# The gate stage of a fused two-model kernel: paced by VectorE's work, shorter look-ups, one-hots shared with ScalarE, and masks added on VectorE

## The chip, the cores and the metric

The kernel runs on one core of one Trainium2 chip. The metric is the device time of one execution in microseconds (us). The kernel before took 3335.89 us as the median of three runs (3335.77 to 3343.4). Every line number "L..." is a line of the kernel before, if nothing else is said.

## The reference

512 tokens of width 1024 pass through five blocks: a mixer of a state-space branch and a forgetting attention, a PEER feed-forward, an even mixer (sparse and differential attention), an odd mixer (compressed, selected and sliding-window attention) and two SwiGLU feed-forwards behind the last two mixers. Two places matter here.

The PEER block scores 8 heads of 2 x 128 keys, takes the best 16 of each half, then the best 16 of the 256 sums, and mixes 128 of 16384 experts per token:

```python
s_top, i_top = lax.top_k(scores, PEER_TOPK)
cand_s = (s_top[..., 0, :, None] + s_top[..., 1, None, :]).reshape(...)
cand_i = (i_top[..., 0, :, None] * PEER_KEYS + i_top[..., 1, None, :]).reshape(...)
best_s, pos = lax.top_k(cand_s, PEER_TOPK)
expert_idx = jnp.take_along_axis(cand_i, pos, axis=-1)
gates = jax.nn.softmax(best_s, axis=-1)
...
act = jax.nn.gelu(jnp.einsum('td,thkd->thk', h_blk, u_sel))
w = (g_blk * act)
return jnp.einsum('thk,thkd->td', w, v_tab[i_blk])
```

The two attentions with plain causal masks are the differential one of the even mixer and the two key branches of the odd one: `s = jnp.where(causal, s, -inf)`, a softmax over the row, and a product with the values.

## The kernel before, in words

Each stream of weights comes in tiles of 128x1024 (512 KB) through one class, `Stream` (from L55 on): a load on SP's queue (L67), a high part of reduced precision made by ScalarE (L75) and the rest made by VectorE (L76). A product is three matmuls, high x high, low x high and high x low (`mm3`, L327 to L330). The program is handed to a scheduler that orders each engine's instructions; every engine then works off its own order.

**PEER** (`peer`, from L932 on). Token block 0 (128 tokens) takes its 128 experts' rows by indirect DMA, one row per token at a time (`gathered`, L967 to L993: POOL issues, VectorE multiplies and sums). The other three blocks (384 tokens) go through all 16384 experts densely, 128 experts at a time: a u pass (`u_pass`, L961) is 24 matmuls over 384 columns that give the activations of 128 experts, and a v pass (`v_pass`, L1182) is 18 matmuls over 512 columns that add their share to the output. Between them the activation is multiplied by the gates, which are zero for all but the chosen experts.

Stage by stage:

- *Query stage.* 16 products, the scores, and `top16` on VectorE.
- *Gate stage.* The first N_SPILL = 80 u passes run ahead of any gate; their activations are parked in DRAM (`spill`, L1132; Gelu on ScalarE at L1138, store at L1140). Beside the first 72 of them the gates are made, in steps of a generator (`all_gates`, L1110): `prep` (L1022) makes for a block of tokens the 50 candidates that can be among the best 16 (their sums `cs` and numbers `ci`), takes the best 16 per head, and looks the numbers up. For the look-up VectorE compares 50 candidates x 16 places (`eq`, L1064), multiplies by the numbers (`pk`, L1066) and sums over the candidates (`ei`, L1067). `build` (L1091) then makes the dense gates, four tokens in a step: one-hots of the second half-key `o2` (L1099) and of the first one times the gate `og` (L1101), both on VectorE, four multiplications of 128x128 on TensorE (L1105), a copy on ScalarE (L1106); a store of 2 MB after each eight steps (L1108). After each parked pass three steps of the generator are taken (`tick`, GATE_RATE = 3), and a step of `all_gates` takes one of `build` and one of `prep` together. Gathers come by `tick(1, ...)`: up to DOTS_C = 20 of 260 in the gate stage.
- *The last eight parked passes* run in the next pools; then come the v passes, 0 to 127. Parked activations and gates are loaded again (L1156), multiplied on POOL (L1163), split (L1166, L1167). Passes 0 to 76 are v passes alone; from there on a u pass stands before each v pass (`peer_order`, L45). The gathers go on beside them at a rate of R_SPILL = 0.7 in the first 80 entries of the order and 1.0 after that.

**Masks.** In `diff_first` (even mixer, L1462; 32 row blocks) and `first` (odd mixer, L1809; 128 row blocks) a row block of scores is two products into one PSUM bank, and between them a third matmul adds the causal mask: identity x mask, in bf16 (L1472, L1819). VectorE takes the negative maximum of the row (L1475, L1821), ScalarE the exponential straight from PSUM (L1477, L1823), and the bank is free after that. The forgetting attention of the first mixer uses another form: one fused operation of VectorE that negates the scores' sum with a second operand and takes the extreme of the row at once, with the sum written to SBUF (L851).

## Time and profile before

| | |
|---|---|
| runs | 3335.77, 3335.89, 3343.4 us |
| the profiled execution | 3341.76 us, its span 3339.6 us |
| TensorE (PE) busy | 3171.5 us, 95% |
| VectorE (DVE) busy | 2242.3 us, 67% |
| ScalarE (ACT) busy | 1345.7 us, 40% |
| GpSimd (POOL) busy | 680.9 us, 20% |
| mean granted clock of TensorE | 0.977 |
| read from HBM, written to it | 474.17 MB, 51.40 MB |

A busy TensorE is not one at its peak: its matmuls are pipelined and their ends are modelled, so rates are read from the starts of rows. Busy shares over the whole span hide the stages; the gate stage lies at about 592 to 1008 us of the span, the v passes from 1050 to about 1800, the even mixer's first attention at about 1920 to 2060 and the odd mixer's at about 2670 to 2940.

### The profile page before, as it was taken

To read this page: it belongs to the slowest core of one execution; us is meant where nothing else is said; L and a number is where in the kernel's file an instruction comes from. 1 tells how busy PE (TensorE), PEld (TensorE's weight loads), DVE (VectorE), ACT (ScalarE), POOL (GpSimd) and SP (SyncE) were. 2 spreads that over 40 slices of the span, in tenths; PEclk is the share of its full clock that TensorE was granted. 3 is DMA by queue.
4 is the path that set the end of the run, shared out by engine and by line. 5 is a ranking of instruction groups with operands and counts; after the bars stand their busy time and mean duration, and the time that the engine had idled before them with its cause. 6 is when DMAs were issued, how large, how long until landed. Compare 5 with 4: busy or idle time off the path is not lost.

```text
span 3339.6 us, 46326 instructions
## 1 busy us (share of the span) xinstructions
PE 3171.5 (95%) x17267; PEld 2759.1 (83%) x17267; DVE 2242.3 (67%) x4704; ACT 1345.7 (40%) x2494; POOL 680.9 (20%) x815
## 2 busy tenths in 40 slices
PE   7989999988999999999999997999999999999999
PEld 6988878988998777899998985878888986778887
DVE  6886349999985787888887787643324377753322
ACT  4445333423443333333334455632322377742322
POOL 1451000010004555566673100000000110000000
PEclk9999999999999999999999997999999998999999
DMA  4223232455669999999997230123233210123232
GB/s 140 79 78 113 95 120 81 154 189 199 237 249 345 321 354 319 319 345 335 340 332 249 70 101 16 42 82 101 95 95 121 83 45 4 55 65 100 95 95 82
DMA packets 226418, 529.25 MB, mean 158 GB/s; under 512 B 19081, under 2 KB 113161, under 8 KB 224273
## 3 DMA queue, kind: packets, MB, share of 16 engines
q1 hardware_dynamic: 186448, 376.32, 33.4%
q0 software_dynamic: 36864, 134.23, 11.2%
q10 hardware_dynamic: 2880, 15.73, 1.2%
q8 instruction: 136, 2.23, 0.3%
q14 instruction: 90, 0.73, 0.1%
HBM read 474.17 MB, written 51.40 MB: 157 GB/s over the span
## 4 chain that ended last, share of the span: by engine, by line
PE 75%; DVE 15%; ACT 3%; DMA 3%; issue 2%; POOL 1%; SPq 0%; ACTq 0%; DVEq 0%; POOLq 0%
PE mm L329 20%; PE mm L328 20%; PE mm L330 19%; DVE wlo L76 3%; PE ax L1105 2%; PE ax L328 2%; PE ax L330 2%; PE ax L329 2%; DMA wraw<-in_peer_v_dram 1%; PE tx L1280 1%; ACT whi L75 1%; DVE ei L1067 1%; PE tx L1840 1%; DVE xn L319 1%; DMA rw<-in_peer_rows_dram,idx 1%
## 5 line engine op out<-in xcount | busy, mean ns | idle before, releaser
L76 DVE TENSOR_TENSOR wlo<-wraw,whi 128x1024 fp32r<-128x1024 f32 x525 | 670.3, 1277 | 573.2 <-ACT whi L75 565.9
L75 ACT CAST whi<-wraw 128x1024 fp32r<-128x1024 f32 x525 | 549.5, 1049 | 1042.3 <-PE mm L329 402.6
L330 PE MATMUL mm<-hhi,wlo 128*128 128x512 f32 (+2 forms) x1608 | 600.0, 374 | 10.2 <-DVE wlo L76 10.1
L328 PE MATMUL mm<-hhi,whi 128*128 128x512 f32 (+2 forms) x1608 | 602.1, 375 | 0.3 <-ACT whi L75 0.3
L329 PE MATMUL mm<-hlo,whi 128*128 128x512 f32 (+2 forms) x1608 | 600.9, 374 | 0.0
L328 PE MATMUL mm<-whi,hhi 128*128 128x256 f32 (+1 forms) x1280 | 382.7, 300 | 9.4 <-DVE vl L272 4.5
L330 PE MATMUL mm<-whi,hlo 128*128 128x256 f32 (+1 forms) x1280 | 380.3, 299 | 3.0 <-DVE hlo L272 2.7
L329 PE MATMUL mm<-wlo,hhi 128*128 128x256 f32 (+1 forms) x1280 | 381.6, 299 | 0.0
L330 PEld LDWEIGHTS mm<-hhi,wlo 128*128 128x128 f32 (+1 forms) x1608 | 303.6, 189 | 52.7 <-DVE wlo L76 12.0
L328 PEld LDWEIGHTS mm<-hhi,whi 128*128 128x128 f32 (+1 forms) x1608 | 304.1, 189 | 41.7 <-ACT hhi L271 0.7
L329 PEld LDWEIGHTS mm<-hlo,whi 128*128 128x128 f32 (+1 forms) x1608 | 303.6, 189 | 40.7 <-DVE hlo L272 0.4
L329 PE MATMUL mm<-wlo,wth 128*128 128x512 f32 x768 | 304.7, 397 | 1.2 <-DVE wlo L76 0.8
L330 PE MATMUL mm<-whi,wtl 128*128 128x512 f32 x768 | 303.6, 395 | 0.0
L975 POOL DMA_INDIRECT rw<-in_peer_rows_dram,idx x128 | 169.9, 1328 | 634.5 <-DVE act L984 377.3
L328 PE MATMUL mm<-whi,wth 128*128 128x512 f32 x768 | 250.8, 400 | 24.0 <-ACT whi L75 24.0
L328 PEld LDWEIGHTS mm<-whi,hhi 128*128 128x128 f32 x1280 | 248.3, 194 | 17.9 <-DVE vl L272 4.7
L330 PEld LDWEIGHTS mm<-whi,hlo 128*128 128x128 f32 x1280 | 246.8, 193 | 9.8 <-DVE hlo L272 3.0
L329 PEld LDWEIGHTS mm<-wlo,hhi 128*128 128x128 f32 x1280 | 248.2, 194 | 6.2 <-issue 0.2
L975 POOL DMA_INDIRECT rw<-in_peer_v_dram,idx x128 | 179.8, 1405 | 96.2 <-DVE acc L992 72.2
L328 PEld LDWEIGHTS mm<-whi,wth 128*128 128x128 f32 x768 | 145.1, 190 | 60.5 <-ACT whi L75 29.8
L1166 ACT CAST wth<-w 128x384 fp32r<-128x384 f32 x128 | 65.8, 514 | 285.4 <-PE mm L329 198.2
L992 DVE SCALAR_TENSOR_TENSOR acc<-rw,act,acc 128x1024 f32<-128x1024 f32 x127 | 176.4, 1389 | 5.7 <-DMA rw<-in_peer_v_dram,idx 4.5
(558 smaller groups left out, 5903.4 us busy)
## 6 DMA issues: line engine op xcount, KB each, us to landing
wraw<-in_peer_u_dram SPq DMA_DIRECT2D x128, 512.0 KB, 4.5
wraw<-in_peer_v_dram SPq DMA_DIRECT2D x128, 512.0 KB, 6.9
gt<-gst SPq DMA_DIRECT2D x12, 2048.0 KB, 7.2
g<-gt SPq DMA_DIRECT2D x32, 768.0 KB, 10.0
wraw<-in_w_gate_dram SPq DMA_DIRECT2D x44, 512.0 KB, 3.4
wraw<-in_w_up_dram SPq DMA_DIRECT2D x44, 512.0 KB, 3.5
wraw<-in_w_down_dram SPq DMA_DIRECT2D x44, 512.0 KB, 3.7
at<-as ACTq DMA_DIRECT2D x20, 768.0 KB, 5.0
```

What stands on the lines that cost most here:

```text
L75: self.nc.scalar.copy(hi[:, :w], r[:, :w])
L76: self.last = self.nc.vector.tensor_sub(lo[:, :w], r[:, :w], hi[:, :w])
L319: V.scalar_tensor_tensor(xn, x[:, o], rs, grow[:, o], op0=ALU.mult, op1=ALU.mult)
L328: PE.matmul(ps, ah, bh, start=start, stop=False)
L329: PE.matmul(ps, ah, bl, start=False, stop=False)
L330: PE.matmul(ps, al, bh, start=False, stop=stop)
L975: G.indirect_dma_start(out=rw, out_offset=None, in_=A[("peer_rows", "peer_v")[m]], in_offset=bass.IndirectOffsetOnAxis(ap=idx[:, k:k + 1], ...
L992: V.scalar_tensor_tensor(acc0, rw, act[:, k:k + 1], acc0, op0=ALU.mult, op1=ALU.add)
L1067: V.tensor_reduce(ei[:, hd], pk.rearrange("p c k -> p k c"), axis=AX.X, op=ALU.add)
L1105: PE.matmul(ps[:, i * P:(i + 1) * P], o2[:, i], og[:, i], start=True, stop=True)
L1166: S.copy(wh, w)
L1280: K["nc"].tensor.transpose(ps[:, t * P:(t + 1) * P], src(t), K["ident"])
```

## The change

1. N_SPILL goes from 80 to 72, so that 64 passes stand in the gate stage and eight more u passes beside v passes. DOTS_C goes from 20 to 28 and R_SPILL from 0.7 to 0.62.
2. A step of the generator now says how much it weighs (1 to 4), `build` and `prep` steps count one by one, and after each parked pass as much weight is taken as spreads all of it over the 64 passes.
3. The look-up of the first eight of 16 places compares only 20 candidates, the second eight all 50: 560 elements instead of 800. The numbers are copied to that list by ScalarE (`cl`, seven copies per block of tokens), and the product is written with the candidates in order, so that the sum reads them in order.
4. Two of four `og` per step are made by ScalarE: an Abs of the difference and a Relu of gate minus gate x difference. The slots are copied by ScalarE, and the negated gate is made by VectorE.
5. The mask matmuls go; VectorE adds the mask in the fused operation and writes the sum to SBUF, and the exponential works there in place. The mask is made once per mixer by POOL and VectorE.

```diff
-N_SPILL = 80
-GATE_RATE = 3
-DOTS_C = 20
+N_SPILL = 72
+DOTS_C = 28
-R_SPILL = 0.7
+R_SPILL = 0.62
...
+            FEW = [(sum(PAIRS[:a]), 8 // (a + 1), 1) for a in range(4)]
+            FEW += [(sum(PAIRS[:4]), 1, 1), (sum(PAIRS[:5]), 3, PAIRS[5])]
+            NF8 = sum(n for _, n, _ in FEW)
+            NL = NF8 + NC
...
-                yield
+                cl = tp.tile([P, 8, NL], F32, tag="cl", bufs=1, name=nm("cl"))
+                lists(S.copy, cl, ci)
+                yield 4
...
-                    eq = tp.tile([P, NC, TOPK], BF16, tag="eq", bufs=1, name=nm("eq"))
-                    V.tensor_tensor(eq, iox, bcast(bp[:, hd], 1, NC), op=ALU.is_equal)
-                    pk = tp.tile([P, NC, TOPK], F32, tag="pk", bufs=1, name=nm("pk"))
-                    V.tensor_mul(pk, eq, bcast(ci[:, hd], 2, TOPK))
-                    V.tensor_reduce(ei[:, hd], pk.rearrange("p c k -> p k c"), axis=AX.X, op=ALU.add)
-                    yield
+                    eq = tp.tile([P, NL, 8], BF16, tag="eq", bufs=1, name=nm("eq"))
+                    pk = tp.tile([P, 8, NL], F32, tag="pk", bufs=1, name=nm("pk"))
+                    halves = [(slice(0, NF8), slice(0, 8)), (slice(NF8, NL), slice(8, 16))]
+                    for c, k in halves:
+                        V.tensor_tensor(eq[:, c], iox[:, c], bcast(bp[:, hd, k], 1, c.stop - c.start), op=ALU.is_equal)
+                    V.tensor_mul(pk.rearrange("p k c -> p c k"), eq, bcast(cl[:, hd], 2, 8))
+                    for c, k in halves:
+                        V.tensor_reduce(ei[:, hd, k], pk[:, :, c], axis=AX.X, op=ALU.add)
+                    yield 2
...
-                sl = tp.tile([P, 3, P], F32, tag="sl", bufs=2, name=nm("sl"))
-                V.tensor_copy(sl.rearrange("p a b -> p (a b)"), ps[:, :3 * P])
-                yield
+                sl = tp.tile([P, 4, P], F32, tag="sl", bufs=2, name=nm("sl"))
+                S.copy(sl[:, :3].rearrange("p a b -> p (a b)"), ps[:, :3 * P])
+                V.tensor_scalar(sl[:, 3], ps[:, 2 * P:3 * P], -1.0, None, op0=ALU.mult)
+                yield 2
...
                         for i in range(4):
-                            V.tensor_scalar(og[:, i], iot, sl[:, 0, t0 + i:t0 + i + 1], sl[:, 2, t0 + i:t0 + i + 1],
-                                            op0=ALU.is_equal, op1=ALU.mult)
+                            e, g, ng = (sl[:, q, t0 + i:t0 + i + 1] for q in (0, 2, 3))
+                            if i % 2:
+                                ds = tp.tile([P, P], F32, tag="ds", bufs=2, name=nm("ds"))
+                                S.activation(ds, iot, AF.Abs, bias=e, scale=-1.0)
+                                S.activation(og[:, i], ds, AF.Relu, bias=g, scale=ng)
+                            else:
+                                V.tensor_scalar(og[:, i], iot, e, g, op0=ALU.is_equal, op1=ALU.mult)
...
-                        yield
+                        yield 1.25
...
                         for g in list(both):
-                            if next(g, 0) == 0:
+                            n = next(g, 0)
+                            if n == 0:
                                 both.remove(g)
-                        yield
+                            else:
+                                yield n
...
+            work = NT * (4 + 8 + 2 + 16) + ND * (2 + 32 * 1.25)
             for e in range(N_SPILL - N_LATE):
                 spill(e, tp)
-                tick(0, GATE_RATE * (e + 1))
+                tick(0, work * (e + 1) / (N_SPILL - N_LATE))
                 tick(1, (e + 1) * DOTS_C // N_SPILL)
...
+def causal_mask(K, pool):
+
+    mk = pool.tile([P, T], F32, name=K["nm"]("mk"))
+    K["nc"].gpsimd.memset(mk[:, :T - P], 0.0)
+    K["nc"].vector.tensor_copy(mk[:, T - P:], K["tri"])
+    return mk
...
                 PE.matmul(ps[:, :N], qr, kh[:, :N], start=True, stop=False)
-                PE.matmul(ps[:, W - P:W], identb, trib, start=False, stop=False)
                 PE.matmul(ps[:, :N], qr, kl[:, :N], start=False, stop=True)
-                V.tensor_reduce(mx[:, r:r + 1], ps[:, :W], axis=AX.X, op=ALU.max, negate=True)
                 p = op.tile([P, W], F32, tag=f"pd{r}", bufs=3 if r > 1 else 2, name=nm("pd"))
-                S.activation(p, ps[:, :W], AF.Exp, bias=mx[:, r:r + 1], accum_out=den[:, r:r + 1])
+                V.tensor_tensor_reduce(p, ps[:, :W], mk[:, T - W:], -1.0, 3.0e38, op0=ALU.add, op1=ALU.min,
+                                       accum_out=mx[:, r:r + 1])
+                S.activation(p, p, AF.Exp, bias=mx[:, r:r + 1], scale=-1.0, accum_out=den[:, r:r + 1])
```

The same edit of the masks is made in `diff_first`.

Three places of the order show how the instructions stand. Lines of the changed kernel are its own: L74 is the split of L75, L1126 the Abs, L1127 the Relu, L1132 the one-hot multiplication of L1105, L1133 the copy of L1106, L1169 the Gelu of L1138.

ScalarE among the one-hot steps, before:

```order
L1106 COPY gst_8048<-ax_8251 128x128x4
L1106 COPY gst_8048<-ax_8269 128x128x4
L75 CAST whi_9924<-wraw_9831 128x1024
L1138 ACTIVATE as_9857<-mm_9891 128x384
L1106 COPY gst_8313<-ax_8321 128x128x4
L1106 COPY gst_8313<-ax_8339 128x128x4
L75 CAST whi_9960<-wraw_9864 128x1024
L1138 ACTIVATE as_9857<-mm_9923 128x384
```

ScalarE at the like place now:

```order
L1126 ACTIVATE ds_9131<-iot,sl_8276 128x128
L1126 ACTIVATE ds_9135<-iot,sl_8276 128x128
L1127 ACTIVATE og_9128<-ds_9131,sl_8276 128x128
L1127 ACTIVATE og_9128<-ds_9135,sl_8276 128x128
L1133 COPY gst_9046<-ax_9058 128x128x4
L1126 ACTIVATE ds_9191<-iot,sl_8276 128x128
L1126 ACTIVATE ds_9195<-iot,sl_8276 128x128
L74 CAST whi_9463<-wraw_9276 128x1024
L1169 ACTIVATE as_9302<-mm_9401 128x384
L1127 ACTIVATE og_9188<-ds_9191,sl_8276 128x128
L1127 ACTIVATE og_9188<-ds_9195,sl_8276 128x128
```

Between two splits of a weight tile ScalarE had a Gelu and two or three copies; now each step brings two Abs and two Relu as well, and some Relu stand behind the next split and the next Gelu.

TensorE at the last one-hot steps, before: they end inside the third last pass of the loop, and two whole passes and the eight late ones follow.

```order
L328 MATMUL mm_10524<-hhi_5370,whi_10456 128x384
L329 MATMUL mm_10524<-hlo_5371,whi_10456 128x384
L1105 MATMUL ax_9706<-og_9700,o_1168_9699 128x128 x4
L330 MATMUL mm_10524<-hhi_5370,wlo_10457 128x384
L328 MATMUL mm_10524<-hhi_5370,whi_10456 128x384
L329 MATMUL mm_10524<-hlo_5371,whi_10456 128x384
L330 MATMUL mm_10524<-hhi_5370,wlo_10457 128x384
L1105 MATMUL ax_9719<-og_9713,o_1171_9712 128x128 x4
L328 MATMUL mm_10524<-hhi_5370,whi_10456 128x384
```

TensorE at the end of the loop now (39 one-hot multiplications stand behind the last pass mm_10788; the first twelve rows from its last matmul on):

```order
L329 MATMUL mm_10788<-hhi_5370,wlo_10619 128x384
L1132 MATMUL ax_10611<-og_10601,o_1351_10600 128x128 x3
L1132 MATMUL ax_10660<-og_10650,o_1357_10649 128x128
L1132 MATMUL ax_10679<-og_10669,o_1363_10668 128x128
L1132 MATMUL ax_10660<-og_10650,o_1357_10649 128x128 x3
L1132 MATMUL ax_10679<-og_10669,o_1363_10668 128x128 x2
L1132 MATMUL ax_10696<-og_10686,o_1368_10685 128x128
L1132 MATMUL ax_10679<-og_10669,o_1363_10668 128x128
L1132 MATMUL ax_10748<-og_10738,o_1375_10737 128x128
L1132 MATMUL ax_10696<-og_10686,o_1368_10685 128x128 x2
L1132 MATMUL ax_10765<-og_10755,o_1380_10754 128x128
L1132 MATMUL ax_10696<-og_10686,o_1368_10685 128x128
```

Before, every one-hot step had matmuls of a pass behind it; now the last ten stand by themselves. From the first of the 384 one-hot multiplications to the last there are 910 matmuls of passes before (37.9 passes) and 835 now (34.8), and 29 whole passes stand ahead of the first one now.

TensorE at a row block of scores in the odd mixer, before:

```order
L1818 MATMUL sx_25321<-kdh_24446,qs_24601 128x256
L1819 LDWEIGHTS identb
L1819 MATMUL sx_25321<-trib,identb 128x128
L1820 MATMUL sx_25321<-kdl_24447,qs_24601 128x256
L1818 MATMUL sx_25328<-kdh_24446,qs_24601 128x384
```

and now:

```order
L1860 MATMUL sx_26585<-kdh_25104,qs_25322 128x512
L1861 MATMUL sx_26585<-kdl_25105,qs_25322 128x512
L1860 MATMUL sx_26636<-kdh_25141,qs_25322 128x256
L1861 MATMUL sx_26636<-kdl_25142,qs_25322 128x256
L1882 MATMUL tx_26556<-ident,pd_26443 128x128
```

Two instructions of TensorE's queue are gone per row block.

## Rows read from the trace of the kernel before

**Rows 1.** The page, part 4: the chain of work that ended last, by engine.

```profile
PE 75%; DVE 15%; ACT 3%; DMA 3%; issue 2%; POOL 1%; SPq 0%; ACTq 0%; DVEq 0%; POOLq 0%
```

**Rows 2.** Busy time by stretch: length, busy us (instructions) per engine, clock, DMA share, GB/s.

```profile
core 0: us, PE busy (x) PEld busy (x) DVE busy (x) ACT busy (x) POOL busy (x), PEclk, DMA share, GB/s
592.00:1008.00 416.00, 397.61 (x2505) 393.72 (x2504) 392.70 (x1081) 171.37 (x254) 26.27 (x19) 0.98 0.59 209
...
725.00:1008.00 283.00, 272.24 (x1800) 269.05 (x1799) 266.67 (x667) 119.15 (x185) 16.18 (x11) 0.98 0.61 220
1050.00:1394.00 344.00, 325.66 (x1374) 257.84 (x1373) 268.09 (x326) 112.22 (x151) 198.24 (x162) 1.00 0.94 335
1394.00:1792.00 398.00, 398.00 (x2002) 360.88 (x2001) 333.82 (x309) 142.70 (x192) 265.40 (x193) 1.00 0.94 335
1920.00:2060.00 140.00, 110.52 (x653) 93.79 (x652) 119.15 (x313) 68.15 (x178) 9.27 (x12) 0.82 0.19 64
2670.00:2940.00 270.00, 254.57 (x1607) 200.01 (x1607) 205.12 (x470) 197.38 (x523) 15.29 (x20) 0.96 0.10 34
```

**Rows 3.** Line 1138, the Gelu: ns min/median/max, first and last start.

```profile
L1138 ACT ACTIVATE as<-mm x72: 476/483/496, 597.1 to 1003.8; 128x384 f32<-128x384 f32 x72
```

**Rows 4.** Timeline of TensorE in a pass: start us, us, engine, line, operation.

```profile
871.50 1.05 PE L1105 MATMUL ax<-og,o 128*128 128x128 f32 x8
...
872.31 0.42 PE L330 MATMUL mm<-hhi,wlo 128*128 128x384 f32 x1
...
873.09 0.34 PE L328 MATMUL mm<-hhi,whi 128*128 128x384 f32 x1
...
875.69 0.33 PE L328 MATMUL mm<-hhi,whi 128*128 128x384 f32 x1
```

**Rows 5.** Groups by line, 592 to 1008 us: count | busy us, mean ns | idle before.

```profile
L1101 DVE TENSOR_SCALAR og<-iot,sl 128x128 f32<-128x128 f32 x384 | 106.4, 339 | 0.0
L76 DVE TENSOR_TENSOR wlo<-wraw,whi 128x1024 fp32r<-128x1024 f32 x72 | 87.8, 1221 | 11.6 <-ACT whi L75 11.6
...
L1067 DVE TENSOR_REDUCE ei<-pk 128x16 f32<-128x800 f32 x32 | 49.5, 1547 | 0.1
L1066 DVE TENSOR_TENSOR pk<-eq,ci 128x800 f32<-128x800 bf16 x32 | 31.7, 992 | 0.1
L1064 DVE TENSOR_TENSOR eq<-iox,bp 128x800 bf16<-128x800 bf16 x32 | 18.3, 571 | 0.0
...
L75 ACT CAST whi<-wraw 128x1024 fp32r<-128x1024 f32 x72 | 75.7, 1052 | 129.5 <-PE mm L329 107.6 <-DMA wraw<-in_peer_u_dram 9.2 <-PE ax L1105 6.8
L1106 ACT COPY gst<-ax 128x512 f32<-128x512 f32 x96 | 56.2, 586 | 104.2 <-PE ax L1105 104.0
```

**Rows 6.** ScalarE: group of line 853; timeline of two neighbours in the late passes.

```profile
L853 ACT ACTIVATE prow<-prow,mx 128x128 f32<-128x128 f32 x8 | 3.2, 403 | 5.0 <-DVE mx L851 5.0
...
1006.96 1.05 ACT L75 CAST whi<-wraw 128x1024 fp32r<-128x1024 f32 x1 [2.72 <-PE ax L329]
1007.92 0.49 ACT L1138 ACTIVATE as<-ax 128x384 f32<-128x384 f32 x1
```

**Rows 7.** DMA from 1050 to 1394 us, all queues.

```profile
DMA packets 54356, 115.24 MB, mean 335 GB/s; under 512 B 3228, under 2 KB 30876, under 8 KB 54335
```

**Rows 8.** Groups by line, 2670 to 2940 us: a maximum over 512 elements in order.

```profile
L1821 DVE TENSOR_REDUCE mx<-sx 128x1 f32<-128x512 f32 x32 | 22.0, 687 | 11.2 <-PE sx L1820 11.0
```

**Rows 9.** Odd mixer: timeline of TensorE; its wait for the score bank (us, times, longest).

```profile
2829.26 0.28 PE L1818 MATMUL sx<-kdh,qs 128*128 128x256 f32 x1
...
2829.62 0.28 PE L1818 MATMUL sx<-kdh,qs 128*128 128x256 f32 x1
...
2830.22 0.28 PE L328 MATMUL mm<-whi,hhi 128*128 128x256 f32 x1
...
2830.34 0.28 PE L329 MATMUL mm<-wlo,hhi 128*128 128x256 f32 x1
...
PE sx L1818 <- ACT pd L1823: 5.7, 11, 1.1
```

**Rows 10.** Line 851, the fused operation of the first mixer: its accumulator read.

```profile
L851 DVE DVE_READ_ACCUMULATOR2_ANT mx<- x32: 71/82/85, 91.6 to 327.1; 128x1 f32 x32
```

More of the change, by code (lines that the diff above doesn't have):

```diff
@@ L1127, in tick @@
                     with tc.issue_after(ws.last.ins) if lane else nullcontext():
-                        if next(lanes[lane], 0) == 0:
-                            lanes[lane] = None
-                    done[lane] += 1
+                        n = next(lanes[lane], 0)
+                    if n == 0:
+                        lanes[lane] = None
+                    done[lane] += n
             def spill(e, pool, bank=bank_m):
```

34 lines of the change are left out of this document (22 added, 12 removed).

## Prediction

> **What bounds the kernel now.** Start with the chain of work that ended last: three quarters of the span is TensorE [rows 1]. So a microsecond counts only if it is taken from TensorE's instructions or from a gap between them, and the busy time by stage tells where gaps are [rows 2]. Four stages matter.
>
> Gate stage (parked passes, 592 to 1008 us): TensorE is busy for 397.6 us and VectorE for 392.7 of 416, while ScalarE has 171.4 [rows 2]. The Gelu that ends a parked pass starts first at 597.1 and for the 72nd time at 1003.8 [rows 3]: 71 intervals of 5.73, about 412 us for 72. What must TensorE do in them? The starts from 873.09 to 875.69 are 15 steps of 0.173, and a pass has 24 matmuls: 4.16 us. One one-hot step (four multiplications, shown as eight) holds the queue from 871.50 to 872.31, 0.81 us [rows 4]. 72 x 4.16 + 96 x 0.81 = 378, so 34 us are lost, partly as gaps, partly as matmuls that run slowly between gaps. VectorE is full; it is what TensorE waits for.
>
> Stage of the v passes alone (1050 to 1394 us): 18.3 us of gaps, VectorE and ScalarE well below full, the DMA engines at 0.94 and 335 GB/s [rows 2, 7]. The transfers bound it.
>
> Stage of u and v passes (1394 to 1792 us): TensorE has no gap at all [rows 2].
>
> Attention: in the odd mixer TensorE is busy for 254.6 of 270 us, VectorE for 205.1, ScalarE for 197.4. In the even mixer's first attention TensorE has 110.5 of 140 at a granted clock of 0.82, VectorE 119.2: there the search for the selected keys on VectorE leads [rows 2].
>
> **The change, part by part.**
>
> *Eight passes fewer in the gate stage.* They are not dropped: they become u passes beside v passes, where TensorE has no gap, so they cost 8 x 4.16 = 33 us there. In the gate stage they take 33 us of TensorE with them, 8 lo splits on VectorE (1.22 each) and 8 hi splits and Gelus on ScalarE (1.05 + 0.48) [rows 3, 5]. The other two parts must bring the profit.
>
> *VectorE in the gate stage.* Half of the first one-hots leave it: half of 106.4 us, 53 [rows 5]. The look-up works on 560 elements instead of 800. Before, its three operations are 0.57 + 0.99 + 1.55 = 3.11 us, 32 times. In proportion to elements they would be 2.18, plus two more instructions of some 0.1: 2.4. The sum over candidates now reads its input in order; a reduction that reads in order takes 0.69 us for 512 elements in the odd mixer [rows 8], so some 0.7 for 560, and the look-up 1.9. Bounds 1.9 and 2.5; I take 2.2, a saving of 29 us. The negated gate and the six gathers more that fall here cost about as much as the eight splits save. VectorE comes to about 392.7 - 53 - 29 = 311 us. TensorE needs 64 x 4.16 + 78 = 344. VectorE no longer leads.
>
> *ScalarE in the gate stage.* It gets 384 activations of 128x128, two for each of 192 one-hots. None such stands in this stage. The nearest rows: an exponential of 128x128 from SBUF with one per-partition operand takes 0.403 us, and a Gelu starts 0.96 us after a split that lasts 1.05, so neighbours overlap by 0.09 [rows 6]. That is 0.31 us in a row of them and 0.40 standing alone; the Relu has two such operands and may be longer. With the seven copies per block of tokens (small), ScalarE has 171.4 - 12 + 119 to 154 + 10 = 288 to 323 us against 344: below TensorE over the whole stage, but not where it matters. The order of the program says where: the one-hot steps stand among 37.9 passes before and 34.8 after, and the first 29 passes have none. In that stretch:
> TensorE 34.8 x 4.16 + 78 = 223.
> VectorE: 266.7 before in that stretch, less 53, less 15 if half of what the look-ups save falls there, less 4 for three splits: about 195.
> ScalarE: 34.8 x (1.05 + 0.48) + 96 x 0.586 [rows 3, 5] = 109, less 0.09 for each of these 166 = 94; with 119 to 154 and some 8 for copies and table loads: 221 to 256.
> So ScalarE and TensorE are level there, and TensorE's order ends with 39 one-hot multiplications behind the last pass, where nothing fills the wait for ScalarE. I take 240 for the stretch, about the middle of ScalarE's range, and 121 + 6 for the 29 passes ahead (6 for the first gathers, which block VectorE's queue when they are late, as before). 367 against 412: 45 saved, 33 paid later, **12 us** gained. Bounds: 29 gained (stretch at TensorE's 223) and 4 lost (stretch at 256).
>
> ScalarE's page in the Trainium skill ("ScalarE: Activation LUTs", section "What ACT_TABLE_LOAD costs") says that each per-partition operand adds about 93 ns, so that a Relu with two would last some 0.49 us; its overlap of 93 ns agrees with the 0.09 of [rows 6]. By that the 384 would be 137 us, an estimate, inside my bounds. Its section "Rules for kernel authors" tells to keep relu on VectorE; that is the third rival.
>
> *Fewer bytes in the v passes.* 69 instead of 77 passes run without a u pass. Each loads a v matrix (0.524 MB), a quarter of a g and of a parked tile (0.197 MB each) and its share of the gathers: before (260 - 20) / (0.7 x 80 + 90) x 0.7 = 1.15 rows of 0.524 MB, after (260 - 28) / (0.62 x 72 + 106) x 0.62 = 0.955. 1.52 MB falls to 1.42 MB. 69 x 1.42 = 98 MB at 335 GB/s is 292 us, and 69/77 of TensorE's 325.7 busy us is 292 too. So the gaps should shrink, though two equal demands never fit without a seam: 18 us of gaps become 6, **12 us** gained; bounds 0 and 18. In the stage of u and v passes the gathers fall from 3.29 to 3.08 per pair, so it stays without gaps.
>
> *Masks.* 160 mask matmuls go, 128 in the odd and 32 in the even mixer. Two 256-column score matmuls with a mask between take 0.36 us from 2829.26 to 2829.62; two such without one take 2 x 0.12 [rows 9]. The mask costs 0.12: 15.4 us in the odd mixer. The score bank is now free after VectorE's pass, not after the exponential: TensorE's waits of 5.7 us for that are open to gain [rows 9]. VectorE pays one accumulator read of 0.08 more per row block [rows 10], 10.5 us beside a VectorE that is 76% busy. I take three quarters of 15.4, **12 us**; bounds 2 and 21. In the even mixer 32 x 0.12 = 4 us of TensorE against 2.6 us on the VectorE that leads: **1 us**, bounds 8 gained and 4 lost.
>
> **Sum.** 12 + 12 + 12 + 1 = 37 us. Against the profiled execution, 3341.8 us, that is 3305. The median of the three runs shown, 3335.9, lies 5.9 below it, so a timed run should give **3299 us**, a ratio of 0.989. About 0.3%, 10 us, can be told from no change.
>
> **Rivals.**
> 1. *The gate stage becomes TensorE's own.* VectorE has slack, ScalarE keeps up because its splits are issued two passes ahead. For it: both engines' sums are at or below TensorE's. Against: three queues in order, and builds denser than before (2.8 steps per pass instead of 2.5). Gate 121 + 223 = 344, that is 68 - 33 = 35 gained; with 18 in the v passes and 17 for masks 70: 3266 us.
> 2. *The pace is not what the scheduler makes of it.* The change wants the building spread by VectorE's work, but the order crowds it into fewer passes than before. Then the 34 us lost stay lost: 344 + 34 = 378, which 33 us later eat up. Left are 12 + 12 + 1 = 25 less a few: 3312 us. Against: what was lost came from VectorE, which is relieved.
> 3. *ScalarE becomes the bound, and the kernel slower.* If its one-hots overlap with nothing, because each Relu waits for its Abs and for the slots, a step takes 0.586 + 2 x 0.40 + 2 x 0.50 = 2.39 us; 96 of them, 53 of splits and Gelus and 8 more are 290 us in the stretch, the stage 417, 5 more than now. With the 33 us moved, less 25 for the rest: 13 us slower, 3349 us. It decides from a step of 2.25 us on. Against: pairs of independent Abs stand in a row in the order, and independent activations did overlap [rows 6].
>
> The State Buffer page of the Trainium skill ("SBUF — State Buffer", section "Door 1: The DMA port swizzle (why `[64,N]` ≈ `[32,N]`)") says that accesses which jump to a new 16-byte line each time pay a penalty. The look-up's sum before reads with such jumps and takes 1.55 us for 800 elements, which agrees; now the product is written with them. By that rule the 0.69 us of the product would grow to some 1.1, an estimate, and VectorE's 195 us in the stretch to some 202: still under TensorE.
>
> **How the numbers follow.** Forecast 0.5, rival 1 0.2, rival 2 0.2, rival 3 0.1. The terms' bounds, not all at one end, carry the forecast from 3275 to 3322. The range takes in most of rival 1 and all of rival 2, and leaves out rival 3: **3260 to 3334**. Faster by over 0.3% (below 3326): the forecast, rival 1 and most of rival 2, 0.85; within 0.3%: 0.07; slower 0.08.
>
> **What would show it.** Right: VectorE in the gate stage falls to about three quarters busy and ScalarE rises to four fifths or more; TensorE's stage from the first to the 64th Gelu takes about 360 us; an Abs lasts 0.39 to 0.41 us; the gaps in the v passes fall to a third at fewer GB per pass; no mask row in TensorE's list and some 12 us less between the odd mixer's first and last score. Wrong: the one-hot multiplications of TensorE wait for ScalarE's rows by some 30 us or more (rival 3), VectorE is still full (the strided product cost more than 2.5 us per look-up), or the stage of u and v passes shows gaps, so that moving eight passes cost more than 33 us.

## Result and profile after

| | before | after |
|---|---|---|
| median, runs of one chip | 3337.28 us (4 runs) | 3297.16 us (3295.19 to 3298.92, 4 runs) |
| ratio | | 0.9879, 95% interval 0.9866 to 0.9892 |
| profiled execution, its span | 3341.8, 3339.6 us | 3298.9, 3296.9 us |

The change makes the kernel 1.2% faster; 3299 had been forecast. The same marks in both traces cut the span into the prediction's stages (us from the span's start):

| mark | before | after | gain so far |
|---|---|---|---|
| first parked Gelu (L1138, now L1169) | 597.1 | 597.7 | -0.6 |
| first of the eight late Gelus | 1007.9 | 959.9 | 48.0 |
| last of them | 1051.2 | 1003.7 | 47.5 |
| first Gelu beside v passes (L1198, now L1230) | 1397.9 | 1302.0 | 95.9 |
| last of these | 1791.9 | 1762.2 | 29.7 |
| table load for the first SwiGLU, behind the even mixer | 2194.9 | 2166.2 | 28.7 |
| table load for the second SwiGLU, behind the odd mixer | 2978.6 | 2935.6 | 43.0 |
| end | 3339.6 | 3296.9 | 42.7 |

Read it with the move in mind. Eight passes left the gate stage and eight v passes left the stage of v passes alone; both stand in the 56 pairs that were 48. The rows of the Gelus in the profile after (duration in ns as min/median/max, then first and last start):

```profile
L1169 ACT ACTIVATE as<-mm x64: 467/483/505, 597.7 to 939.7; 128x384 f32<-128x384 f32 x64
...
L1169 ACT ACTIVATE as<-ax x8: 482/486/487, 959.9 to 1003.7; 128x384 f32<-128x384 f32 x8
```

```profile
L1230 ACT ACTIVATE a<-ax x56: 478/487/492, 1302.0 to 1762.2; 128x384 f32<-128x384 f32 x56
```

55 intervals in 460.2 us are 8.37 each; before, 47 in 394.0 were 8.38. So eight pairs more cost 67 us; at the prediction's 4.16 us a u pass is half of a pair, so 33.5 are counted for the u passes and 33.5 for the v passes. The gate stage (first to first late Gelu) fell from 410.8 to 362.2; 48.6 less the 33.5 paid later is **15 gained**. The v passes alone fell from 346.7 to 298.3; 48.4 less the 33.5 that only moved is **15 gained**. The odd mixer gained **14**, the even mixer lost **1**, the rest is under 1 us in each stage.

Busy time by stretch, with the columns of [rows 2]:

```profile
592.00:713.00 121.00, 117.23 (x674) 116.02 (x673) 117.58 (x467) 54.56 (x91) 16.26 (x11) 1.00 0.59 205
713.00:955.00 242.00, 237.23 (x1615) 233.89 (x1614) 203.65 (x492) 230.93 (x561) 16.56 (x14) 1.00 0.67 240
1004.00:1302.00 298.00, 291.30 (x1249) 235.12 (x1248) 230.06 (x271) 101.40 (x135) 153.19 (x133) 0.99 0.94 331
1302.00:1762.00 460.00, 460.00 (x2311) 416.70 (x2310) 377.90 (x370) 166.97 (x230) 290.19 (x214) 1.00 0.93 330
1887.00:1994.00 107.00, 90.03 (x570) 80.96 (x568) 98.25 (x268) 57.88 (x146) 8.94 (x10) 0.87 0.19 60
1994.00:2037.00 43.00, 17.11 (x86) 14.47 (x85) 24.13 (x86) 12.84 (x38) 2.40 (x4) 0.68 0.19 63
2641.00:2879.00 238.00, 223.00 (x1414) 182.78 (x1413) 199.09 (x580) 190.29 (x503) 15.08 (x19) 0.96 0.10 34
```

Ahead of the first one-hot multiplication VectorE is still full (117.6 of 121). From the first to the last (713 to 955) it is not, 203.7 of 242, but ScalarE nearly is, 230.9, and TensorE shows 237.2. The same stretch in three parts:

```profile
713.00:825.00 112.00, 111.47 (x753) 110.54 (x752) 111.97 (x297) 105.60 (x255) 8.53 (x7) 1.00 0.64 228
825.00:944.00 119.00, 117.61 (x817) 117.17 (x816) 86.95 (x184) 114.91 (x279) 8.04 (x7) 1.00 0.70 251
944.00:960.00 16.00, 13.16 (x79) 11.18 (x78) 4.73 (x12) 12.02 (x31) 0.00 (x0) 1.00 0.63 256
```

VectorE stays full up to 825 us, then ScalarE is the fuller one. TensorE has hardly a gap as long as passes fill its queue; its gaps stand at the end, where 39 one-hot multiplications follow the last pass. Its waits for the two helpers, from 713 to 955 us (us in total, times, longest), are far below the 30 us that rival 3 needed:

```profile
PE ax L1132 <- DVE og L1129: 2.7, 4, 1.4
PE ax L1132 <- ACT og L1127: 1.8, 6, 0.5
```

The v passes alone have 6.7 us of gaps, where they had 18.3. The two lines of the even mixer, the scores and what follows them, come back below: while the scores are issued TensorE idles for 17 of 107 us, and behind the last score it works for 17 of 43 at a granted clock of 0.68.

The groups of the gate stage, 592 to 960 us (count | busy us, mean ns of one | idle before), against [rows 5]; first over all engines, then VectorE's look-up by shape:

```profile
L1127 ACT ACTIVATE og<-ds,sl 128x128 f32<-128x128 f32 x192 | 87.0, 493 | 2.2 <-DVE sl L1108 2.2
...
L1126 ACT ACTIVATE ds<-iot,sl 128x128 f32<-128x128 f32 x192 | 70.5, 401 | 0.0
...
L1120 DVE TENSOR_TENSOR o<-iot,sl 128x512 f32<-128x512 f32 x96 | 67.2, 700 | 32.9 <-PE ax L1132 32.9
L1129 DVE TENSOR_SCALAR og<-iot,sl 128x128 f32<-128x128 f32 x192 | 58.6, 354 | 0.0
L1133 ACT COPY gst<-ax 128x512 f32<-128x512 f32 x96 | 55.4, 578 | 6.0 <-PE ax L1132 5.7
```

```profile
L1085 DVE TENSOR_TENSOR pk<-eq,cl 128x560 f32<-128x560 bf16 x32 | 38.7, 1210 | 0.1
...
L1087 DVE TENSOR_REDUCE ei<-pk 128x8 f32<-128x400 f32 x32 | 18.4, 576 | 0.0
...
L1084 DVE TENSOR_TENSOR eq<-iox,bp 128x400 bf16<-128x400 bf16 x32 | 12.0, 375 | 0.0
...
L1087 DVE TENSOR_REDUCE ei<-pk 128x8 f32<-128x160 f32 x32 | 10.5, 329 | 0.2
...
L1084 DVE TENSOR_TENSOR eq<-iox,bp 128x160 bf16<-128x160 bf16 x32 | 7.9, 247 | 0.0
```

Who waits has turned round: VectorE's second one-hots now wait 32.9 us for TensorE, and ScalarE's copy out of the bank, which waited 104 us for it [rows 5], waits 5.7. The look-up is 2.74 us by the sum of these durations (0.62, 1.21, 0.91), not 2.2: the product on fewer elements is longer than the 0.99 of [rows 5].

### The profile page after: what moved, and what is told of

Its sections match the earlier page's. It is cut to its first block, busy times and chain, and to the rows that moved or that the text cites. A ratio compares the mean times of both kernels' runs of the same rounds, so it can differ in the third digit from the quotient of the medians.

```text
span 3296.9 us, 46594 instructions
## 1 busy us (share of the span) xinstructions
PE 3138.6 (95%) x17107; PEld 2747.8 (83%) x17107; DVE 2172.4 (66%) x4738; ACT 1478.0 (45%) x2918; POOL 669.7 (20%) x817
## 4 chain that ended last, share of the span: by engine, by line
PE 83%; DVE 11%; ACT 2%; DMA 2%; issue 1%; POOL 0%; SPq 0%; DVEq 0%; ACTq 0%; POOLq 0%
PE mm L327 21%; PE mm L328 21%; PE mm L329 21%; PE ax L327 3%; PE ax L329 3%; PE ax L328 3%; PE ax L1132 2%; DVE wlo L75 2%; PE tx L1312 1%; PE tx L1882 1%; DMA wraw<-in_peer_v_dram 1%; PE po L1892 1%; DVE tl L271 1%; DVE xn L318 1%; PE sx L1860 1%
## 5 line engine op out<-in xcount | busy, mean ns | idle before, releaser
L75 DVE TENSOR_TENSOR wlo<-wraw,whi 128x1024 fp32r<-128x1024 f32 x525 | 664.0, 1265 | 565.7 <-ACT whi L74 558.2
L74 ACT CAST whi<-wraw 128x1024 fp32r<-128x1024 f32 x525 | 549.4, 1049 | 958.0 <-PE mm L328 319.9
L329 PE MATMUL mm<-hhi,wlo 128*128 128x512 f32 (+1 forms) x1544 | 576.8, 374 | 2.8 <-DVE wlo L75 2.7
L327 PE MATMUL mm<-hhi,whi 128*128 128x512 f32 (+1 forms) x1544 | 577.9, 376 | 0.2 <-ACT hhi L270 0.2
L328 PE MATMUL mm<-hlo,whi 128*128 128x512 f32 (+1 forms) x1544 | 577.7, 374 | 0.0
L329 PEld LDWEIGHTS mm<-hhi,wlo 128*128 128x128 f32 x1544 | 289.9, 188 | 44.1 <-DVE wlo L75 3.6
L327 PEld LDWEIGHTS mm<-hhi,whi 128*128 128x128 f32 x1544 | 290.4, 188 | 41.6 <-ACT hhi L270 0.8
L328 PEld LDWEIGHTS mm<-hlo,whi 128*128 128x128 f32 x1544 | 289.9, 188 | 40.6 <-DVE hlo L271 0.4
L974 POOL DMA_INDIRECT rw<-in_peer_rows_dram,idx x128 | 161.9, 1265 | 568.6 <-DVE act L983 344.1
L327 PE MATMUL mm<-whi,wth 128*128 128x512 f32 x768 | 258.6, 399 | 12.9 <-ACT whi L74 12.9
L1198 ACT CAST wth<-w 128x384 fp32r<-128x384 f32 x128 | 65.8, 514 | 310.3 <-PE mm L328 159.7
L983 DVE CUSTOM_DVE_ANT_0 rw<-rw,hrow 128x1024 f32<-128x1024 f32 x128 | 178.8, 1405 | 12.9 <-DMA rw<-in_peer_rows_dram,idx 12.9
```

What stands on the lines that cost most here:

```text
L74: self.nc.scalar.copy(hi[:, :w], r[:, :w])
L75: self.last = self.nc.vector.tensor_sub(lo[:, :w], r[:, :w], hi[:, :w])
L327: PE.matmul(ps, ah, bh, start=start, stop=False)
L328: PE.matmul(ps, ah, bl, start=False, stop=False)
L329: PE.matmul(ps, al, bh, start=False, stop=stop)
L974: G.indirect_dma_start(out=rw, out_offset=None, in_=A[("peer_rows", "peer_v")[m]], in_offset=bass.IndirectOffsetOnAxis(ap=idx[:, k:k + 1], ...
```

## Experiments

Each kernel was timed in five rounds against the kernel before. Times are medians.

### One-hots: all on VectorE, or three of eight on ScalarE

```diff
-                            if i % 2:
+                            if False:                          # all on VectorE
+                            if i == 1 or i == 3 and t1 % 8:    # three of eight on ScalarE
```

> The changed kernel with all first one-hots on VectorE, as before. From the first one-hot multiplication to the last, 242 us now, VectorE has 204 us and ScalarE 231; 192 one-hots more are 59 us of VectorE (58.6 for the 192 it has) and 157 less of ScalarE. Theory (VectorE becomes what TensorE waits for again, 262 us and its seams): the stretch 265 to 272, the kernel 23 to 30 us slower than the changed one, about 3323. Rival (TensorE's own 223 to 237 us set the stretch and the spread decides): at most 8 us slower, 3305 or less.

3304.5 us, ratio 0.9903 (0.9888 to 0.9918): 7 slower than the changed kernel, inside the rival's bound, though not by its mechanism. The rows of the parked Gelus:

```profile
L1169 ACT ACTIVATE as<-mm x64: 477/482/497, 601.1 to 924.9; 128x384 f32<-128x384 f32 x64
...
L1169 ACT ACTIVATE as<-ax x8: 477/483/487, 975.1 to 1018.2; 128x384 f32<-128x384 f32 x8
```

The gate stage did get longer, 374.0 instead of 362.2, at its end: the passes are through at 924.9 and one-hot steps follow for 44 us more. In TensorE's order 116 one-hot multiplications now stand behind the last pass, where there were 39, and there TensorE waits for VectorE, as the theory had it:

```profile
925.00:975.00 50.00, 37.03 (x254) 32.79 (x254) 43.55 (x131) 18.19 (x32) 0.00 (x0) 1.00 0.47 194
```

```profile
PE ax L1132 <- DVE og L1129: 12.3, 25, 1.2
```

The theory overrated the size: the stretch took 251 us (718.0 to 968.8), not 265 to 272. And the v passes behind it took 290.9 instead of 298.3 (last late Gelu 1018.2, first Gelu beside v passes 1309.1). So 7 of the 12 us came back. Halving the one-hots is worth 7 us, not the tens that 53 us of VectorE suggest. Of these 7 the trace shows the 4 to 5 that the two stages leave; the traced execution took 3311.1 and was already 3.4 us late at its first parked Gelu.

> The changed kernel with three of eight first one-hots on ScalarE instead of four. ScalarE falls by 39 us (48 pairs of 0.40 and 0.49) to 192 in the stretch of 242 us, VectorE rises by 15 to 218, TensorE's own sum is 223. Theory (ScalarE at 96% sets the stretch's second half): 6 to 12 us faster than the changed kernel, 3285 to 3291. Rival 1 (TensorE sets it already): within 3 us of 3297. Rival 2 (VectorE's order, not its sum, is what TensorE waits for next): 5 us or more slower.

3287.7 us, ratio 0.9855 (0.984 to 0.987): 9.5 faster than the changed kernel, the theory. Its busy time from 712 to 945 us, the stretch with one-hot multiplications:

```profile
712.00:945.00 233.00, 232.80 (x1611) 232.11 (x1611) 214.44 (x538) 200.69 (x463) 16.07 (x14) 1.00 0.68 244
```

The stretch fell from 242 to 233, TensorE has no gap left, and both helpers have some 20 to 30 us to spare. Only 12 one-hot multiplications stand behind the last pass in TensorE's order, where there were 39: at half, ScalarE was too full to finish the one-hots beside the passes. The gate stage as a whole fell by less than its stretch, from 362.2 to 357.4; the rest shows in the late passes (41.9 instead of 43.8) and in the v passes alone (295.1 instead of 298.3), where two executions of one order can differ by 3 us (the changed kernel and the one with the mask tile moved, below). So 5 of the 9.5 us are shown to come from the gate stage.

### The look-up: 800 elements; the product in order; both sides in order

For 800 elements the look-up is that of the kernel before, without the copied lists. For the product in order:

```diff
-pk = tp.tile([P, 8, NL], F32, ...)
-V.tensor_mul(pk.rearrange("p k c -> p c k"), eq, bcast(cl[:, hd], 2, 8))
-V.tensor_reduce(ei[:, hd, k], pk[:, :, c], ...)
+pk = tp.tile([P, NL, 8], F32, ...)
+V.tensor_mul(pk, eq, bcast(cl[:, hd], 2, 8))
+V.tensor_reduce(ei[:, hd, k], pk[:, c].rearrange("p c k -> p k c"), ...)
```

> The changed kernel with the look-ups among 800 elements, as before (no copies of the lists on ScalarE). Three operations of 0.57, 0.99 and 1.55 us, 3.11 instead of 2.74 by the sum of their durations: 12 us more of VectorE over 32 look-ups, some 10 us less of ScalarE. Theory (the shorter look-ups are worth little: their strided product cost more than I had taken, and in the stretch with one-hots ScalarE leads): at most 5 us slower than the changed kernel, 3297 to 3302. Rival (VectorE, busy for 117.6 of the 121 us ahead of the first one-hot multiplication, sets that part): the first one-hot multiplication 6 us or more later against the first Gelu and the kernel 6 to 12 us slower, 3303 to 3309.

3311.7 us, ratio 0.9924 (0.991 to 0.9937): 14.5 slower, more than the rival. The first one-hot multiplication and the late Gelus in this kernel:

```profile
L1112 PE MATMUL ax<-og,o x768: 270/275/579, 730.2 to 971.1; 128*128 128x128 f32 x192
...
L1149 ACT ACTIVATE as<-ax x8: 479/483/487, 979.6 to 1022.3; 128x384 f32<-128x384 f32 x8
```

The first one-hot multiplication starts at 730.2 instead of 713.5 and the gate stage takes 382.7 (596.9 to 979.6), 20.5 longer; the v passes alone, 291.2, give 7 back. So the shorter look-up counts where VectorE is full, ahead of the first one-hots. It shows in the scheduler's order: 33.1 passes instead of 29.2 stand ahead of the first one-hot multiplication, and 99 multiplications instead of 39 behind the last pass.

> The changed kernel with the look-up's product written in order and read with jumps by the sum, as before the change, still among 560 elements. Theory (a strided write costs the product half a microsecond, a strided read costs the sum less): the product 0.70 us (0.99 x 560/800) instead of 1.21, the sums 1.09 (1.55 x 560/800) instead of 0.905, 0.33 us less per look-up and 10 us of VectorE; the kernel 0 to 6 us faster than the changed one, 3291 to 3297. Rival (the sum pays more for its jumps than the product saves): sums above 1.42 us and no gain or a loss.

3299.6 us, ratio 0.989 (0.9874 to 0.9905): no gain. The look-up by shape in this kernel:

```profile
L1087 DVE TENSOR_REDUCE ei<-pk 128x8 f32<-128x400 f32 x32 | 29.4, 920 | 0.0
...
L1085 DVE TENSOR_TENSOR pk<-eq,cl 128x560 f32<-128x560 bf16 x32 | 23.5, 734 | 0.1
L1087 DVE TENSOR_REDUCE ei<-pk 128x8 f32<-128x160 f32 x32 | 14.4, 452 | 0.2
...
L1084 DVE TENSOR_TENSOR eq<-iox,bp 128x400 bf16<-128x400 bf16 x32 | 11.4, 358 | 0.0
...
L1084 DVE TENSOR_TENSOR eq<-iox,bp 128x160 bf16<-128x160 bf16 x32 | 7.3, 230 | 0.0
```

The product is 0.73, as the theory had it, so the jumps of the write cost 0.48 us. The sums are 1.37 instead of 0.91: the jumps of the read cost 0.47. That is the rival's outcome, with sums just under its 1.42. TensorE's order has the same 29.2 passes ahead of the one-hots and the same 39 multiplications behind the passes as in the changed kernel. The change had moved one price from the sum to the product.

```diff
-eq = tp.tile([P, NL, 8], ...)
-V.tensor_tensor(eq[:, c], iox[:, c], bcast(bp[:, hd, k], 1, n), ...)
+eq = tp.tile([P, 8, NL], ...)
+V.tensor_tensor(eq[:, :, c], bcast(iox[:, c], 1, 8), bcast(bp[:, hd, k], 2, n), ...)
+V.tensor_mul(pk, eq, bcast(cl[:, hd], 1, 8))
```

> The kernel of the run before this one, with the look-up laid out by slot and then candidate, so that the comparison, the product and the sum all go through memory in order. Theory (each jump costs what the two look-up runs showed, 0.48 us of the product or 0.47 of the sums): comparison 0.62, product 0.73, sums 0.91, 2.26 us instead of 2.74 and 15 us less of VectorE; as the run with 800 elements lost 14 us for 11 of VectorE, the kernel 5 to 12 us faster than that run, 3266 to 3273. Rival 1 (the comparison with an operand that stands still along the inner dimension pays instead): comparison above 1.0 us and no gain. Rival 2 (VectorE no longer sets anything): the durations as in the theory, but within 3 us of that run.

3278.3 us, ratio 0.9826 (0.9813 to 0.9839), against 3277.6 of the run it builds on ("both edits" below): the same. The comparison in this kernel:

```profile
L1084 DVE TENSOR_TENSOR eq<-iox,bp 128x400 bf16<-128x400 bf16 x32 | 18.4, 574 | 0.0
...
L1084 DVE TENSOR_TENSOR eq<-iox,bp 128x160 bf16<-128x160 bf16 x32 | 10.3, 321 | 0.0
```

It takes 0.90 instead of 0.62, product and sums 0.74 and 0.88: 2.52 in all, 7 us less of VectorE and not 15. Half of the saving went into the comparison, whose second operand now stands still along the inner dimension; that it is this operand, and not another part of the new layout, was not tested by itself. What was left bought no time, as rival 2 had it. But the scheduler's order changed too: 32.4 passes instead of 29.2 stand ahead of the first one-hot multiplication (at 723.9 us instead of 714.0 in "both edits") and 56 multiplications instead of 12 behind the last pass. So this run does not show that VectorE's time has no worth left.

### The move: undone, alone, and carried on

> The changed kernel with the move undone: 80 parked passes, 20 rows gathered beside them, 0.7. Theory: 8 passes more in the gate stage cost at least 8 x 4.16 = 33 us there, and the same 33 are saved beside the v passes; the v passes alone carry 1.52 instead of 1.42 MB each and get back the 15 us of gaps that went: 12 to 18 us slower than the changed kernel, 3309 to 3315. Rival 1 (a pass in the gate stage still costs 5.4 us): 25 us slower, 3322. Rival 2 (the gaps were the look-ups' and one-hots' doing, not the bytes'): within 4 us of 3297.

3310.2 us, ratio 0.992 (0.9906 to 0.9933): 13 slower, the theory (the traced execution took 3306.6). The gate stage is 30.7 longer for eight passes (597.6 to 990.5), and the v passes alone show their gaps again, 16.2 us of 344:

```profile
1033.00:1377.00 344.00, 327.84 (x1391) 261.54 (x1390) 267.51 (x328) 112.47 (x152) 203.58 (x161) 0.99 0.94 339
```

```diff
-N_SPILL = 80, DOTS_C = 20, R_SPILL = 0.7
+N_SPILL = 72, DOTS_C = 28, R_SPILL = 0.62     # in the kernel before
```

> The kernel before with the move alone: 72 parked passes, 28 rows gathered beside them, 0.62; old look-ups, all one-hots on VectorE, mask multiplications. Theory (VectorE sets the gate stage, so eight passes take only what they have of VectorE with them, 8 x 1.22 us, to some 25 at most as the run with all one-hots on VectorE suggests): gate 10 to 25 shorter, 33 paid beside the v passes, 15 back there: from 8 slower to 7 faster than before, 3329 to 3344. Rival (each pass takes its 5.73 us with it): 46 - 33 + 15 = 28 faster, 3309.

3334.2 us, ratio 0.999 (0.9982 to 0.9999): 3 us. The Gelus:

```profile
L1138 ACT ACTIVATE as<-mm x64: 475/483/496, 600.4 to 914.6; 128x384 f32<-128x384 f32 x64
...
L1138 ACT ACTIVATE as<-ax x8: 478/482/487, 997.3 to 1040.9; 128x384 f32<-128x384 f32 x8
```

Eight passes fewer shorten the gate stage from 410.8 to 396.9 alone: 14 us, not 46. The passes end early, at 914.6, and VectorE needs 80 us more for the one-hots: 192 of the 384 multiplications stand behind the last pass. From 915 to 997 VectorE is busy for 75.9 of 82 us and TensorE for 60.2:

```profile
915.00:997.00 82.00, 60.18 (x403) 52.91 (x403) 75.85 (x231) 28.61 (x50) 0.00 (x0) 0.98 0.46 190
```

The v passes alone take 292.0 (1040.9 to 1332.9) instead of 346.7: 33.5 of it moved, 21 are won. With the 33.5 paid for the u passes 2 us are left. So the same move is worth 3 us here and 13 once VectorE is relieved.

> The kernel with both edits that gained (mask tile moved, three of eight one-hots on ScalarE) and the move carried on: 64 parked passes, 36 rows gathered beside them, 0.54. Theory (the move pays only while TensorE is what the gate stage lasts for): 33 us go from TensorE there, but VectorE keeps 218 - 10 and ScalarE 204 - 12 us in the stretch with one-hots, so the stage gets 10 to 15 us shorter; 33 are paid beside the v passes and at most 9 of gaps are left there to win: 9 to 23 us slower than with 72, 3287 to 3301. Rival (every pass takes its 5.4 us with it and the v passes get their seams back): 10 us faster, 3268.

3310.4 us, ratio 0.9926 (0.9913 to 0.994): 33 slower than with 72 and the same edits (3277.6), beyond the theory's 23. The gate stage fell by 12.1 to 346.2, inside the 10 to 15; 175 one-hot multiplications stand behind the last pass, and TensorE's one-hot multiplications now wait for VectorE:

```profile
PE ax L1132 <- DVE og L1129: 14.6, 29, 0.9
```

(us in total, times, longest.) Most of the miss of 10 us is in the v passes alone: they fell by 27.0 (985.5 to 1252.2) where 33.5 moved away, so 6.5 were lost there instead of won. Another 2 are in the late passes (42.8 instead of 40.6).

### The masks: alone, and the place of the mask tile

The first of these puts the masks of the change into the kernel before and leaves all else.

> The kernel before with the masks alone (both attention mixers), everything else as before. In the changed kernel's trace the odd mixer ended some 14 us sooner against its start and the even mixer about 1 us later. Theory (the terms add up): 13 us faster than before, about 3324 us. Rival (the score stretches tell the worth: 8 us sooner at the last score of the even mixer, 21 in the odd one, and what is given back later belongs to other parts of the change): some 25 us or more faster, 3312 us or less.

3331.3 us, ratio 0.9983 (0.9974 to 0.9993): 5 us, less than either. In its trace the odd mixer is 15.8 shorter (767.9 between the two table loads instead of 783.7) and the even mixer 6.0 longer (409.0 from the last Gelu to the first table load instead of 403.0). The two make 10; 4 of them were lost ahead of the first parked Gelu (601.3 instead of 597.1), where nothing is changed, in a traced execution that took 3338.6, 7 above the median. So the 5 us are less certain than the two stages' own numbers. What the even mixer loses stands on SP's queue. The reload of the residual stream, first in the kernel before, then in the changed one:

```profile
1988.20 1.76 SPq L443 DMA_DIRECT2D xr<-x_sc  x4
```

```profile
2021.91 1.76 SPq L442 DMA_DIRECT2D xr<-x_sc  x4
2023.71 1.21 SPq L1609 DMA_DIRECT2D uk<-in_ev_w_uk_dram  x2
```

Before, it was issued 47 us ahead of the last score (2035.2); now 28 behind it (1994.1), as with the masks alone (2059.9, last score 2032.1). The mask tile adds 2 KB to the pool of the first attention, which then ends 192 bytes inside the place of the residual stream, and SP now waits there for the transposition that reads the pool's last tile. The 2.1 MB go out just ahead of the first loads of the latent heads, and TensorE waits for these:

```profile
PE mm L1654 <- ACT uk L1612: 6.2, 1, 6.2
```

```diff
-        mk = causal_mask(K, dpl)
+        mk = causal_mask(K, rp)      # even mixer: the pool of the rotation tables
```

> The changed kernel with the even mixer's mask tile in the pool of the rotation tables instead of the pool of the first attention; order of the program unchanged. Theory: in the first attention's pool the 2 KB of the mask reach into the place of the residual stream, so its reload (2.1 MB) is issued only after the last transposition (2021.9 us) and goes ahead of the loads of the latent heads; in the other pool it is issued before the last score again, as in the kernel before, and TensorE does not wait 6.2 us for the first of these heads: 6 to 12 us faster than the changed kernel, 3285 to 3291. Rival: the search on VectorE and the transposition behind it set the end of this part, wherever the tile lies: 3297, unchanged.

3287.4 us, ratio 0.9855 (0.984 to 0.987): 9.8 faster, in the theory's range. The reload is back at its place, and the wait at the latent heads fell to 1.6:

```profile
1991.15 1.76 SPq L442 DMA_DIRECT2D xr<-x_sc  x4
```

```profile
PE mm L1654 <- ACT uk L1612: 1.6, 1, 1.6
```

From the last Gelu to the first table load this kernel takes 397.9 instead of 404.0, and all of that lies behind the last score (166.0 instead of 172.1), so 6 of the 9.8 us are shown to come from there. The wait at the latent heads is 4.6 of them. The scheduler also ordered this mixer's instructions anew, against what the expectation says, and the rest may come from that. The five kernels with the tile elsewhere take 396.7 to 397.9 us here, the seven with masks and the tile in the first attention's pool 402.2 to 409.0. The other 4 us lie ahead of this mixer, where the order of the program is the same, and have no cause that the traces show: differences of some 4 us in those stages can be scatter.

> The kernel before with the masks alone and the even mixer's mask tile in the pool of the rotation tables. The masks alone gave 5 us (3331.3 against 3336.5): in that profile the odd mixer is 16 us shorter and the even mixer 6 longer. Theory (the even mixer's loss is the late reload): 6 to 10 us faster than the masks alone, ratio to before 0.995 to 0.9965, some 3320 to 3325. Rival (the masks' worth in this program is 5 us wherever the tile lies): ratio 0.998 to 0.999.

3317.5 us, ratio 0.9939 (0.9926 to 0.9953): 14 faster than with the tile in the other pool, more than the theory's 10, and 19 faster than before. The even mixer takes 396.8, 6 less than before instead of 6 more, the odd one 766.7. The mechanism is the theory's and its size in the even mixer is 12, all behind the last score (162.7 instead of 175.3).

### Both edits that gained

> The changed kernel with both edits that gained: the even mixer's mask tile in the pool of the rotation tables, and three of eight first one-hots on ScalarE. They lie in different stages. Theory (they add up, 9.8 and 9.5 us): 3278. Rival (part of either came from the stages behind it, as the transfers of the v passes give back what the gate stage loses): 3282 or more.

3277.6 us, ratio 0.982 (0.9806 to 0.9833). They add up, and this is the fastest version found, 20 us below the changed kernel.

## Why the prediction was right, and where a term was off

**The bound.** That TensorE's gate stage waited for VectorE held, and the run with the move alone shows it best: eight passes of TensorE taken out, 14 us gained.

**Gate stage, 45 forecast, 48.6 measured.** The stretch with one-hots was to take 240 and took 242; the passes ahead of it 127 and took 116. ScalarE's sum was to be 221 to 256 and is 231; VectorE's 195, and is 204. An Abs lasts 401 ns (0.39 to 0.41 forecast), a Relu 493. The estimate of 0.49 us, from the 0.403 us with one per-partition operand and the 93 ns that the Trainium skill ("ScalarE: Activation LUTs", section "What ACT_TABLE_LOAD costs") gives for each more, agrees with the trace. The same page's section "Rules for kernel authors" in the Trainium skill tells to use VectorE for relu, since per element it is up to about 3 times faster in bf16. Here the numbers have 32 bits, and the trace agrees on the single one-hot, 354 ns on VectorE against 401 and 493 on ScalarE; for the kernel it does not hold: all on VectorE was 7 us slower than half on ScalarE, and three of eight was the best of the shares run.

TensorE's own sum for the stretch, 223, was too low. With three of eight, and with the move undone, the stretch has no gap and takes 232.7 and 271.7 us; less 4.16 for each of its 34.8 and 43.9 passes, a one-hot step is 0.92 and 0.93 us, not the 0.81 of [rows 4]. The forecast of 240 did not rest on that term, as ScalarE's was above it; its better bound, 29 gained, and rival 1 did.

Two marks that I gave for this stage were badly put. VectorE did not fall to three quarters but to 321 of 368 us (my own sum, 311 of 367, said as much), and 360 us was the way to the first late Gelu, not to the 64th, which comes after 342. ScalarE rose to 287 of 368, just under the four fifths.

**The step that failed: the look-up's price.** I took 2.2 us with bounds of 1.9 and 2.5, because the sum now reads in order; it is 2.74, outside. The write with jumps was only in the rivals' part of the prediction, from 0.69 to some 1.1 us. It is 0.73 in order and 1.21 with jumps, so this price belonged into the sum. The State Buffer page of the Trainium skill ("SBUF — State Buffer", section "Door 1: The DMA port swizzle (why `[64,N]` ≈ `[32,N]`)") says that an access which crosses to a new 16-byte line pays a penalty; the traces agree, with 0.48 us more for the write and 0.47 for the read. VectorE saved 12 us by durations, not 29. The forecast survived, as a look-up of 2.74 still leaves VectorE at 204 in the stretch. The sign that I had set for this, a look-up above 2.5 us with VectorE still full, came half: VectorE is full ahead of the one-hots and up to 825 us, and the run with 800 elements shows that its time is worth something there.

**Rival 1 (TensorE's own stage).** Nearly: its stage was 344, the run with three of eight comes to 357.4 with a TensorE that has no gap in the stretch. **Rival 2 (the pace).** Half of it is true: with every step counted as one, the order of the instructions on all five engines is that of the changed kernel, so the weights of the pace move nothing, the scheduler places the steps. But the lost time did not stay. **Rival 3 (ScalarE the bound).** It leads by the 9 us that three of eight took from the stretch, 5 of them kept in the stage, not by the 50 of the rival: its activations do overlap. Two pairs in the timeline of ScalarE after (start us, us):

```profile
901.48 0.70 ACT L1126 ACTIVATE ds<-iot,sl 128x128 f32<-128x128 f32 x2
...
902.55 0.89 ACT L1127 ACTIVATE og<-ds,sl 128x128 f32<-128x128 f32 x2
```

Two Abs in a row take 0.70 us, not 0.80, and two Relus 0.89, not 0.99.

**Eight passes cost 33 us beside the v passes.** Measured 67 for eight pairs, half of it 33.5, with no gap in 460 us. That held, and so did the bytes: 98.53 MB in the 69 v passes alone are 1.43 MB each (1.42 forecast), 116.54 in 77 were 1.51.

**V passes, 12 forecast, 15 measured.** Gaps of 18 were to become 6 and are 6.7. The run with the move undone has them back, and the move alone, with all else as before, has 2.3. Where the gaps lie, in two lines of before and two of after:

```profile
1050.00:1100.00 50.00, 47.10 (x202) 37.24 (x200) 34.17 (x44) 15.99 (x23) 29.50 (x26) 1.00 0.98 356
1100.00:1394.00 294.00, 278.56 (x1173) 220.60 (x1174) 233.92 (x283) 96.24 (x129) 168.74 (x137) 0.99 0.93 331
```

```profile
1005.00:1055.00 50.00, 43.44 (x177) 33.88 (x176) 31.49 (x39) 14.64 (x20) 24.71 (x23) 0.97 0.92 326
1055.00:1300.00 245.00, 244.86 (x1057) 198.58 (x1058) 197.05 (x231) 85.61 (x114) 126.54 (x109) 1.00 0.95 334
```

Before, 15 of 18 us lie behind the first 50; these are gone. What is left stands in the first 50 us, where the transfers run at 326 GB/s and ran at 356 before. That remainder differs from kernel to kernel: with 72 parked passes the stage takes 291 or 292 us with all on VectorE, 800 elements or the move alone, 293 to 295 in the kernels with three of eight, 297 to 299 in the changed kernel, with the mask tile moved and with the product in order. The length of the stage ahead does not order these (374 to 397, 356 to 358 and 362 to 367 us). Why is open; no run separated it.

**Masks, 12 and 1 forecast, 14 and -1 measured.** The odd mixer's scores take 20.8 us less from first to last, but 6.5 come back behind them. The even mixer's small term came from weighing TensorE's gain against VectorE's loss, with bounds of 8 and -4; the runs show that the mask tile's place costs 6 to 12 us there, mostly through a transfer that it makes late. The number is near for another reason, which is luck: with the tile elsewhere the even mixer gains 5 to 6. Its scores then still give back part of what they gain: first to last they take 8.5 us less, and behind them 6.3 more than before in the changed kernel with the tile moved.

**The sum.** The four terms came to 43 us where 37 had been forecast, against a kernel before of 3337.3 (four runs) where 3335.9 (three) had been taken. That 3299 met 3297 within 2 us is in part luck: three terms were 2 or 3 us too small and the fourth 2 too large, and the medians gained 40.1 us, 3 less than the traced executions.

## What to carry to other kernels

A move of work between stages is priced by what bounds each stage at that time: the same eight passes were worth 3 us while VectorE was full, 13 once it was relieved, and the next eight cost 33. A new tile has a second price beside its own work: what lies in the pool that it enlarges, and which transfer then waits for it. When work is shared between two helpers, take the share that leaves the leader without gaps, not half; what counts here is how little of the shared work is left behind the last pass (39 multiplications at half, 12 at three of eight, 116 at none).

## What was not expected of the hardware

The three layouts of one look-up of 560 elements cost 2.74, 2.69 and 2.52 us: a write with jumps adds 0.48 us to the product, a read with jumps 0.47 to the sums, and the layout without either adds 0.27 to the comparison of 16-bit numbers (0.90 instead of 0.62 us), where an operand then stands still along the inner dimension. Much of a jump saved in one operation came back in its neighbour.
